# The attention half of an output projection by Strassen's algorithm (one core, fp32 products in three passes)

## The chip, the cores and the metric

One NeuronCore of a Trainium2 chip runs the whole program. The metric is device microseconds of one execution, lower is better. Engines are named as in the profile: PE (matrix products), DVE (vector), ACT (scalar), POOL (GpSimd), SP (it issues most DMAs).

## The reference

A hybrid encoder block on x (512 positions by 2048), cut to what matters here:

```
h   = rmsnorm(x, norm1_g)
z   = h @ w_in
attn = windowed_gqa(q, k, v, sink)        # 512 x 1024, 8 heads of 128
gm   = chunked_spatial_gating(zg, ...)    # 512 x 1024, 8 groups of 128
mix = concat(rmsnorm(attn, attn_out_norm_g), rmsnorm(gm, gmlp_out_norm_g))
x   = x + mix @ w_out                     # w_out: 2048 x 2048
x   = x + conv_ffn(rmsnorm(x, norm2_g), w_up, conv_w, conv_b, w_down)
out = rmsnorm(x, final_g)
```

The first 1024 rows of `w_out` meet the attention branch, the other 1024 the gating branch. All is float32.

## The kernel before

**Three passes.** Every float32 operand of a large product is split in two parts, `hi` (an ACT cast, `nc.scalar.copy`) and `lo` (a DVE subtraction), and `mm3` (lines 81 to 83) issues three 128x128 by 128x512 matmuls: hi by hi, hi by lo, lo by hi. Weights come from memory in tiles of 128x1024 (512 KB) into a ring of six buffers, the pool `raw`. Their split parts go into the pool `wp`, three buffers for `hi` and three for `lo`. `weights` (line 68) does it all for one tile: SP's load, ACT's cast, DVE's subtraction.

**Order of the program.** Input projection and attention; values of the gating branch; `u` projection (four steps of `tiles_A`, each followed by the gating of two groups); output projection; then an up projection and a down projection that run interleaved, the down one by Strassen's algorithm already (tiles `dp`); final norm.

**The stretch of the change.** `project(half, src, c, r)` (line 413) makes one block of 512 output columns: 4 tiles of weights, 4 row blocks, 96 matmuls into four PSUM banks (tiles `pj`), then one DVE instruction for each row block (line 427) that adds bank times row scale to the residual. Half 0 is attention (columns c = 0 to 3, scale `ra`), half 1 gating (scale `rg`). While half 0 runs, SP also loads the 16 residual blocks `x2[t][c]` of 128x512 (line 425). The attention activations are split once, `ats` (lines 363 to 369).

**What sets the order.** A framework builds the program, orders each engine's instructions by its own plan, and puts a semaphore wait where a tile is read or its buffer reused. Each engine runs its list in order, so one that waits holds up all behind it; SP's list of DMA issues too. The pool `big` has 64 slots of 128x512; a slot comes free when the last reader of its tile is done.

Of the kernel before, what the change touches and what calls it, by code (L numbers as in the profile page):

```python
# [24 lines left out]
H = 8  # L25
KV = 2
# [19 lines left out]


@with_exitstack
def hymba_block(ctx, tc, xT, x, w_in, w_up, w_out, w_down, wsT, cols, brow, frow, srow, rel, out):
# [163 lines left out]
    kk = {}  # L213
# [33 lines left out]
    pst = [psm.tile([P, 256], F32, tag="m", name=f"va_{t}") for t in range(NT)]  # L247
    for u in range(4):
        hi, lo = next_in()
        hv = hi.rearrange("p (k c) -> p k c", k=4)  # L250
        lv = lo.rearrange("p (k c) -> p k c", k=4)
        for t in range(NT):
            for k in range(4):
                kt = u * 4 + k
                a = tuple(z[:, t * P : (t + 1) * P] for z in xs[kt])
                mm3(pst[t], a, (hv[:, k, :], lv[:, k, :]), kt == 0, kt == KT - 1)
    for t in range(NT):
        if t % 2 == 0:
            vh, vl = slot(F32R, f"vah{t}"), slot(F32R, f"val{t}")
        hi, lo = (z[:, (t % 2) * 256 : (t % 2 + 1) * 256] for z in (vh, vl))  # L260
# [4 lines left out]
    at = [slot(F32, f"at{h}") for h in range(H)]  # L265
# [85 lines left out]
    for t in range(NT):  # L351
        for c in range(2):
            v = vg[2 * t + c].rearrange("p (g c) -> p g c", c=P)
            i = t * NG + 4 * c
# [5 lines left out]
        nc.sync.dma_start(ws[i], wsT[:, 4 * i : 4 * i + 4, :].rearrange("p g c -> p (g c)"))  # L360
        nc.sync.dma_start(gb[i], brow[i * S : (i + 1) * S].partition_broadcast(P))

    atg = [[oct.tile([P, 4, S], F32R, tag="oct", name=f"ats{z}{g}") for z in "hl"] for g in range(KV)]
    ats = []
    for h in range(H):
        hi, lo = (z[:, h % 4, :] for z in atg[h // 4])
        nc.scalar.copy(hi, at[h])
        nc.vector.tensor_tensor(lo, at[h], f(hi), op=ALU.subtract)
        ats.append((hi, lo))

    ra = row_stat(asq, 1024, "ra")
    ug = {}
# [13 lines left out]
    def gating(h):  # L386
        ps = pss.tile([P, S], F32, tag="s", name=f"gv{h}")
        for n in range(NT):
            v = vg[2 * n + h // 4][:, (h % 4) * P : (h % 4 + 1) * P]
            nc.tensor.matmul(ps[:, n * P : (n + 1) * P], v, ws[h // 4][:, (h % 4) * P : (h % 4 + 1) * P], start=True, stop=True)  # L390
        t = slot(F32, f"gt{h}")
        bb = gb[h // 4][:, (h % 4) * P : (h % 4 + 1) * P].unsqueeze(1).broadcast_to([P, NT, P])
        nc.vector.scalar_tensor_tensor(
            t.rearrange("p (n c) -> p n c", c=P), ps.rearrange("p (n c) -> p n c", c=P),
            col[:, C_GV + h : C_GV + h + 1], bb, op0=ALU.mult, op1=ALU.add)
        nc.vector.tensor_tensor(t, t, ug[h], op=ALU.mult)
        if h == 0:
# [12 lines left out]

    x2 = [[slot(F32, f"x2_{t}{c}") for c in range(4)] for t in range(NT)]

    def project(half, src, c, r):
        pst = [psm.tile([P, S], F32, tag="m", name=f"pj{half}{c}{t}") for t in range(NT)]
        for u in range(4):
            hi, lo = weights(w_out[(half * 4 + c) * 4 + u], f"o{half}{c}{u}")
# [12 lines left out]
    for c in range(4):  # L429
        project(0, ats, c, ra)  # L430
    rg = row_stat(gsq, 1024, "rg")
    gms = [split(gm[h], f"gm{h}s", scale=col[:, C_GM + h : C_GM + h + 1]) for h in range(NG)]
    ss2 = const.tile([P, 4 * NT], F32, name="ss2")
    hs = []
    for c in range(4):
        project(1, gms, c, rg)
# [271 lines left out]
    for t in range(NT):  # L708
# [19 lines left out]
        for c in (1, 0, 3, 2):  # L728
            o = x2[t][c]
# [21 lines left out]
def _layout(x, norm1_g, w_in, gmlp_v_norm_g, gmlp_ws, gmlp_b, attn_sink, attn_out_norm_g,  # L751
            gmlp_out_norm_g, w_out, norm2_g, w_up, conv_w, conv_b, w_down, final_g):
    x = np.asarray(x)[0]
    wi, wo, wu, wd = (np.asarray(a)[0] for a in (w_in, w_out, w_up, w_down))
    q, k, v = wi[:, :1024], wi[:, 1024:1280], wi[:, 1280:1536]
    u, gv = wi[:, 1536:2560], wi[:, 2560:]
    w1 = np.concatenate([
        _units(np.concatenate([k, q[:, :256]], 1), 512), _units(q[:, 256:512], 256), _units(v, 256),
        _units(q[:, 512:], 256), _units(gv, 512), _units(u, 256)])
    gu = np.concatenate([wu[:, :DFF].reshape(D, NCT, 1, P), wu[:, DFF:].reshape(D, NCT, 1, P)], 2)  # L760
    w2 = _units(gu.reshape(D, 2 * DFF), 256)
    w3 = np.concatenate([_units(wo[:1024], 512), _units(wo[1024:], 512)])
# [10 lines left out]
    return {  # L773
        "xT": np.ascontiguousarray(x.T).reshape(KT, P, S),
        "x": x,
        "w_in": w1, "w_up": w2, "w_out": w3, "w_down": w4,
        "wsT": np.ascontiguousarray(np.asarray(gmlp_ws)[0].transpose(2, 0, 1)),
        "cols": np.ascontiguousarray(cols),
        "brow": np.asarray(gmlp_b)[0].reshape(-1),
        "frow": np.asarray(final_g),  # L780
        "srow": np.asarray(attn_sink)[0],
        "rel": rel,
    }
# [17 lines left out]
```

## Time and profile before

| what | value |
|---|---|
| median of 3 runs | 1943.1 us (1942.53 to 1944.31) |
| the profiled execution | 1942.97 us, span 1941.2 us |
| PE busy in the span | 1929.4 us (99%) |
| DVE, ACT, POOL busy | 63%, 36%, 5% |
| attention's half of the projection | 364.4 to 451.6 us |
| DMA, mean over the span | 120 GB/s |

The span runs from the first to the last instruction; the execution's own time is 1.8 us more. The median of the runs is within 0.2 us of the profiled execution. Times of the trace are microseconds from the span's start.

### The profile page before, as it was taken

What the parts mean: (1) busy time and instruction counts of PE and PEld (TensorE: products, weight loads), DVE (VectorE), ACT (ScalarE), POOL (GpSimd) and SP (SyncE); (2) the same over time, 40 slices, a digit from 0 to 9 for tenths busy, and PEclk for the clock granted to TensorE, in tenths of its full rate; (3) what the DMA queues carried; (4) which work ended last, traced back from release to release, by engine and by line L of the source; (5) the groups of instructions that cost most, each with busy time, mean ns of one, the idle gap of its engine ahead of it and who ended that gap; (6) DMA issues with size and microseconds to landing.
All of it is one profiled execution on the core that took longest, in us unless ns stands there. A gap on an engine that the chain in (4) does not pass through costs nothing.

```text
span 1941.2 us, 22114 instructions
## 1 busy us (share of the span) xinstructions
PE 1929.4 (99%) x8776; PEld 1601.8 (83%) x8776; DVE 1219.1 (63%) x1652; ACT 694.7 (36%) x915; POOL 91.1 (5%) x105
## 2 busy tenths in 40 slices
PE   9999999999999999999999999999999999999998
PEld 8988888888888888888888888888888888888886
DVE  7476573444444767667566666676665757667857
ACT  6243442322332334333233333333333334333334
POOL 5001100100000000000000000000000000000000
PEclk9999999999999999999999999999999999999999
DMA  7212232522223344433444344434444344444432
GB/s 259 97 66 75 68 115 91 174 98 88 92 93 108 109 129 129 128 118 123 133 132 129 115 125 141 130 108 131 131 130 130 109 131 128 133 123 129 132 127 87
DMA packets 68104, 232.54 MB, mean 120 GB/s; under 512 B 7696, under 2 KB 7968, under 8 KB 68000
## 3 DMA queue, kind: packets, MB, share of 16 engines
q1 hardware_dynamic: 62064, 209.87, 31.8%
q0 software_dynamic: 5792, 20.99, 6.6%
q8 instruction: 68, 1.11, 0.2%
q10 hardware_dynamic: 144, 0.26, 0.0%
q14 instruction: 36, 0.29, 0.0%
HBM read 226.90 MB, written 4.19 MB: 119 GB/s over the span
## 4 chain that ended last, share of the span: by engine, by line
PE 98%; DVE 1%; ACT 0%; DMA 0%; issue 0%; ACTq 0%; POOL 0%; POOLq 0%; DVEq 0%
PE up L83 16%; PE up L82 16%; PE up L81 16%; PE dp L81 7%; PE dp L82 7%; PE dp L83 7%; PE pj L81 3%; PE pj L83 3%; PE pj L82 3%; PE g L82 2%; PE g L83 2%; PE g L81 2%; PE u L81 2%; PE u L83 1%; PE u L82 1%; PE vg_ps L81 1%
## 5 line engine op out<-in xcount | busy, mean ns | idle before, releaser
L83 PE MATMUL up<-h_h,lo_u 128*128 128x512 f32 x1408 | 547.9, 389 | 0.0
L81 PE MATMUL up<-h_h,hi_u 128*128 128x512 f32 x1408 | 547.9, 389 | 0.0
L82 PE MATMUL up<-h_l,hi_u 128*128 128x512 f32 x1408 | 547.8, 389 | 0.0
L82 PEld LDWEIGHTS up<-h_l,hi_u 128*128 128x128 f32 x1408 | 264.4, 188 | 54.8
L81 PEld LDWEIGHTS up<-h_h,hi_u 128*128 128x128 f32 x1408 | 264.4, 188 | 54.8
L83 PEld LDWEIGHTS up<-h_h,lo_u 128*128 128x128 f32 x1408 | 264.4, 188 | 54.7
L460 ACT CAST hi_u<-st_u 128x1024 fp32r<-128x1024 f32 x176 | 185.7, 1055 | 323.5 <-PE dp L83 180.6
L461 DVE TENSOR_TENSOR lo_u<-st_u,hi_u 128x1024 fp32r<-128x1024 f32 x176 | 215.2, 1223 | 116.8 <-ACT hi_u L460 116.8
L461 DVE TENSOR_TENSOR lo_b<-st_d,hi_b 128x1024 fp32r<-128x1024 f32 x60 | 73.4, 1223 | 145.6 <-ACT hi_b L460 145.6
L568 DVE TENSOR_TENSOR x<-x,dp 128x512 f32<-128x512 f32 x200 | 136.1, 682 | 1.4
L460 ACT CAST hi_b<-st_d 128x1024 fp32r<-128x1024 f32 x60 | 63.3, 1055 | 179.7 <-PE up L82 175.0
L77 DVE TENSOR_TENSOR lo_i<-st_i,hi_i 128x1024 fp32r<-128x1024 f32 (+1 forms) x57 | 72.0, 1264 | 70.8 <-ACT hi_i L76 70.7
L487 ACT ACTIVATE c<-a,col 128x512 f32<-128x512 f32 x88 | 71.2, 809 | 118.5 <-DVE a L484 118.4
L461 DVE TENSOR_TENSOR lo_t<-st_d,hi_t 128x1024 fp32r<-128x1024 f32 x40 | 48.9, 1223 | 88.6 <-ACT hi_t L460 88.6
L76 ACT CAST hi_i<-st_i 128x1024 fp32r<-128x1024 f32 (+1 forms) x57 | 58.8, 1032 | 119.8 <-PE u L82 38.7
L77 DVE TENSOR_TENSOR lo_o<-st_o,hi_o 128x1024 fp32r<-128x1024 f32 x32 | 39.2, 1225 | 95.5 <-ACT hi_o L76 95.5
L81 PE MATMUL dp<-hi_t,afs 128*128 128x512 f32 x240 | 93.4, 389 | 0.0
L82 PE MATMUL dp<-lo_t,afs 128*128 128x512 f32 x240 | 93.4, 389 | 0.0
L83 PE MATMUL dp<-hi_t,afs 128*128 128x512 f32 x240 | 93.4, 389 | 0.0
L549 POOL DMA_DIRECT2D st_t<-in_w_down x40 | 34.8, 869 | 1237.0 <-DMA st_t<-in_w_down 860.0
L489 DVE SCALAR_TENSOR_TENSOR c<-a,col,c 128x511 f32<-128x511 f32 x88 | 66.1, 751 | 41.5 <-ACT c L487 41.2
L460 ACT CAST hi_t<-st_d 128x1024 fp32r<-128x1024 f32 x40 | 42.2, 1054 | 109.0 <-PE up L82 105.2
(288 smaller groups left out, 3226.6 us busy)
## 6 DMA issues: line engine op xcount, KB each, us to landing
st_u<-in_w_up SPq DMA_DIRECT2D x176, 512.0 KB, 3.2
st_d<-in_w_down SPq DMA_DIRECT2D x60, 512.0 KB, 3.3
st_i<-in_w_in SPq DMA_DIRECT2D x55, 512.0 KB, 3.3
st_t<-in_w_down SPq DMA_DIRECT2D x40, 512.0 KB, 3.3
st_t<-in_w_down POOLq DMA_DIRECT2D x40, 512.0 KB, 5.4
st_o<-in_w_out SPq DMA_DIRECT2D x32, 512.0 KB, 3.2
xg<-in_xT SPq DMA_DIRECT2D x16, 256.0 KB, 6.4
x<-in_x SPq DMA_DIRECT2D x16, 256.0 KB, 5.6
```

Source lines behind the costliest of these rows:

```text
L76: nc.scalar.copy(hi[:, cs], st[:, cs])
L77: nc.vector.tensor_tensor(lo[:, cs], st[:, cs], f(hi[:, cs]), op=ALU.subtract)
L81: nc.tensor.matmul(ps, a[0], b[0], start=start, stop=False, skip_group_check=free)
L82: nc.tensor.matmul(ps, a[0], b[1], start=False, stop=False, skip_group_check=free)
L83: nc.tensor.matmul(ps, a[1], b[0], start=False, stop=stop, skip_group_check=free)
L460: nc.scalar.copy(hi, st)
L461: nc.vector.tensor_tensor(lo, st, f(hi), op=ALU.subtract)
L487: nc.scalar.activation(t, a, AF.Identity, scale=w[1], bias=col[:, C_CB + j * 44 + i : C_CB + j * 44 + i + 1])
L489: nc.vector.scalar_tensor_tensor(t[:, 1:], a[:, : S - 1], w[0], t[:, 1:], op0=ALU.mult, op1=ALU.add)
L549: nc.gpsimd.dma_start(t, src(*y), accum_op=ALU.add)
L568: nc.vector.tensor_tensor(d, d, ps, op=op)
```

## The change

Attention's half of the projection becomes two runs of `attn_out(m)`. Run m makes the output columns of blocks m and m + 2 by the Winograd form of Strassen's algorithm: rows in two halves (256 each), the 1024 inner elements in two halves of four heads, columns in two halves. Seven products stand where the plain form has eight. A product is two half-products of 12 matmuls (`mm3` four times, 128x512 each): 2 x 7 x 24 = 336 matmuls in place of 384. The products are, in order: `b11`, `t3`, `b21`, `t4`, `t1`, `t2`, `b22`.

- Weights: `b11`, `b21`, `b22` are quarters of the weights, loaded. `t3` and `t1` are a load plus a second DMA, issued by POOL, that adds another quarter (line 468 of the new file). `t2` and `t4` are DVE additions (line 478). `b11` and `t3` lie in the ring `raw` (two tiles of 512 KB each), the rest in slots of `big` (four loads of 256 KB each).
- Activations: `at_forms(k)` makes the seven forms for one pair of heads on DVE and ACT, in pieces of 128x256. Forms 0 and 1 follow the gating of u step 2, forms 2 and 3 that of step 3.
- Results: product 1 is copied to `acco` by ACT; `into` (line 502) adds PSUM times row scale to two residual blocks; `attn_sums` (line 542) adds `acco` later, within `project`, which now does the gating half only.
- Residual blocks: eight pairs, each just ahead of the product that needs it.

```
-    atg = [[oct.tile([P, 4, S], F32R, tag="oct", name=f"ats{z}{g}") for z in "hl"] for g in range(KV)]
-    for h in range(H):
-        nc.scalar.copy(hi, at[h])
-        nc.vector.tensor_tensor(lo, at[h], f(hi), op=ALU.subtract)
...
+    def at_forms(k):
+        c = S // 2
+        a11, a21, a12, a22 = at[k][:, :c], at[k][:, c:], at[4 + k][:, :c], at[4 + k][:, c:]
+        def put(name, v):
+            hi, lo = atf[name][k][:, :c], atf[name][k][:, c:]
+            nc.scalar.copy(hi, v)
+            nc.vector.tensor_tensor(lo, v, f(hi), op=ALU.subtract)
+        put("11", a11)
+        put("12", a12)
+        put("22", a22)
+        t = slot(F32, f"ats{k}")
+        d, e = t[:, :c], t[:, c:]
+        nc.vector.tensor_tensor(d, a11, a21, op=ALU.subtract)
+        put("s3", d)
+        nc.vector.tensor_tensor(e, a22, a21, op=ALU.subtract)
+        put("s1", e)
+        nc.vector.tensor_tensor(d, e, a11, op=ALU.add)
+        put("s2", d)
+        nc.vector.tensor_tensor(e, d, a12, op=ALU.subtract)
+        put("s4", e)
...
+        if q >= 2:
+            at_forms(2 * q - 4)
+            at_forms(2 * q - 3)
...
+        def plus(x_, y_, name, ring=False):
+            ts, parts = blocks(name, ring)
+            for t, s_ in zip(ts, chunks(*x_, len(ts))):
+                nc.sync.dma_start(t, s_)
+            for t, s_ in zip(ts, chunks(*y_, len(ts))):
+                nc.gpsimd.dma_start(t, s_, accum_op=ALU.add)
+            return parts
...
+        def product(a, ts, name, ps, start):
+            for kk in range(2):
+                hi = wp.tile([P, 1024], F32R, tag="whi", name=f"ohi_{name}{m}{kk}")
+                lo = wp.tile([P, 1024], F32R, tag="wlo", name=f"olo_{name}{m}{kk}")
+                for k in range(2):
+                    cs, st = slice(k * S, (k + 1) * S), ts[2 * kk + k]
+                    nc.scalar.copy(hi[:, cs], st)
+                    nc.vector.tensor_tensor(lo[:, cs], st, f(hi[:, cs]), op=ALU.subtract)
...
+        b11 = q(0, 0, True)
+        t3 = plus((1, 1), (0, 1), "t3", True)
+        residual(1, 1)
+        pa = bank(psm, "m", "op1")
+        product("11", b11, "b11", pa, True)
+        for t in range(2):
+            nc.scalar.copy(acco[m][t], pa[t])
+        b21 = q(1, 0)
+        residual(0, 0)
+        pb = bank(pss, "s", "op7")
+        product("s3", t3, "t3", pb, True)
+        into(1, 1, pb, nra)
+        t1 = plus((0, 1), (0, 0), "t1")
+        residual(1, 0)
+        product("12", b21, "b21", pa, False)
+        into(0, 0, pa, ra)
+        t2 = add(b11, t3)
+        t4 = add(b21, t2)
+        product("22", t4, "t4", pb, False)
+        into(1, 0, pb, ra)
+        b22 = q(1, 1)
+        residual(0, 1)
+        pa = bank(psm, "m", "op5")
+        product("s1", t1, "t1", pa, True)
...
-            if half == 0:
-                nc.sync.dma_start(x2[u][c], x[u * P : (u + 1) * P, c * S : (c + 1) * S])
+            if u == 0:
+                attn_sums(c)
...
-    for c in range(4):
-        project(0, ats, c, ra)
+    for m in range(2):
+        attn_out(m)
...
+    w3 = wo[:1024].reshape(2, 4, P, 2, 2, 512).transpose(4, 0, 3, 2, 1, 5).reshape(8, P, 2048)
+    w3g = _units(wo[1024:], 512)
```

**How it moves instructions, place 1: SP's list where the projection begins.** In the names `st_o` are weights of the projection before, `x2` residual blocks (row, column), `owq` and `owt` the new weight tiles: the digits of `owt310` are t3, run 1, tile 0, of `owq1000` b21, run 0, tile 0. Before, SP had:

```order
L75 DMA st_o020_3311<-in_w_out 128x1024
L425 DMA x2_00_3027<-in_x 128x512
L425 DMA x2_10_3031<-in_x 128x512
L425 DMA x2_20_3035<-in_x 128x512
L425 DMA x2_30_3039<-in_x 128x512
L425 DMA x2_01_3028<-in_x 128x512
```

At the same place it now has:

```order
L466 DMA owt310_3453<-in_w_out 128x1024
L466 DMA owt311_3454<-in_w_out 128x1024
L474 DMA x2_22_3109<-in_x 128x512
L474 DMA x2_32_3113<-in_x 128x512
L460 DMA owq1000_3173<-in_w_out 128x512
L460 DMA owq1001_3174<-in_w_out 128x512
L460 DMA owq1002_3175<-in_w_out 128x512
L460 DMA owq1003_3176<-in_w_out 128x512
L474 DMA x2_00_3099<-in_x 128x512
```

The weights of product 3 (`owq1000` to `owq1003`) stand behind the ring loads of the other run's t3, whose second one, `owt311`, needs the ring buffer that t3 of run 0 (`owt301`) leaves.

**Place 2: SP's list ahead of the third product of run 1.** The list before has no such tiles; after `x2_33` it held only `st_o` loads. Now:

```order
L75 DMA st_o02_3896<-in_w_outg 128x1024
L75 DMA st_o03_3926<-in_w_outg 128x1024
L460 DMA owq1010_3501<-in_w_out 128x512
L460 DMA owq1011_3502<-in_w_out 128x512
L460 DMA owq1012_3503<-in_w_out 128x512
L460 DMA owq1013_3504<-in_w_out 128x512
L474 DMA x2_01_3100<-in_x 128x512
L474 DMA x2_11_3104<-in_x 128x512
L466 DMA owt110_3551<-in_w_out 128x512
```

`st_o03`, a weight tile of the gating half, takes the ring buffer of `owt311` (t3 of run 1), and b21 and t1 of run 1 (`owq101x`, `owt11x`) are queued behind it.

**Place 3: PE's list at the start of product 4 of run 1.** `op710` and `op711` are the two banks of products 2 and 4, `op510` the first bank of product 5, `ohi` and `olo` the split weights:

```order
L81 MATMUL op710_3511<-ohi_t410_3611,atf22_2383 128x512
L81 MATMUL op711_3512<-ohi_t410_3611,atf22_2383 128x512
L81 MATMUL op510_3659<-ohi_t110_3661,atfs10_2384 128x512
L82 MATMUL op710_3511<-olo_t410_3612,atf22_2383 128x512
L83 MATMUL op710_3511<-ohi_t410_3611,atf22_2383 128x512
```

One matmul of product 5, which reads t1's first tile, stands in the list after two of product 4's 24.

## Rows read from the trace of the kernel before

**Rows 1.** The page, part 1: busy time, share of the span, instructions of each engine.

```profile
PE 1929.4 (99%) x8776; PEld 1601.8 (83%) x8776; DVE 1219.1 (63%) x1652; ACT 694.7 (36%) x915; POOL 91.1 (5%) x105
```

**Rows 2.** Windows: length, busy us (instructions) of each engine, PE clock, DMA share, GB/s.

```profile
364.40:451.60 87.20, 87.20 (x389) 72.22 (x387) 37.29 (x43) 22.00 (x25) 3.10 (x2) 1.00 0.44 145
...
364.40:386.00 21.60, 21.60 (x98) 17.92 (x97) 9.63 (x13) 6.27 (x8) 3.10 (x2) 1.00 0.83 275
386.00:451.60 65.60, 65.60 (x292) 54.30 (x291) 27.66 (x32) 15.73 (x17) 0.00 (x0) 1.00 0.31 102
```

**Rows 3.** Tile pj: ns min/median/max of one, first and last start in us.

```profile
L81 PE MATMUL pj<-hi_o,atsh x128: 389/389/476, 364.4 to 450.9; 128*128 128x512 f32 x128
L82 PE MATMUL pj<-lo_o,atsh x128: 389/389/395, 364.7 to 451.1; 128*128 128x512 f32 x128
L83 PE MATMUL pj<-hi_o,atsl x128: 389/389/393, 365.0 to 451.3; 128*128 128x512 f32 x128
```

**Rows 4.** Groups of instructions by form: busy us, mean ns of one, idle before.

```profile
L81 PE MATMUL dp<-hi_t,afs 128*128 128x512 f32 x240 | 93.4, 389 | 0.0
...
L568 DVE TENSOR_TENSOR accu<-accu,dp 128x512 f32<-128x512 f32 x80 | 53.8, 684 | 1.1
...
L427 DVE SCALAR_TENSOR_TENSOR x<-pj,ra_r,x 128x512 f32<-128x512 f32 x16 | 11.6, 747 | 3.2 <-PE pj L83 3.2
...
L610 DVE TENSOR_TENSOR x<-x,dn 128x256 f32<-128x256 f32 x8 | 3.3, 418 | 1.1 <-PE dn L83 0.9
...
L521 ACT CAST afs<-s 128x512 fp32r<-128x512 f32 x40 | 24.8, 620 | 31.2 <-DVE s L512 31.2
```

**Rows 5.** DVE's timeline: start, us, what.

```profile
316.69 1.23 DVE L77 TENSOR_TENSOR lo_i<-st_i,hi_i 128x1024 fp32r<-128x1024 f32 x1
...
364.95 0.74 DVE L393 SCALAR_TENSOR_TENSOR gt<-gv,col,gb 128x512 f32<-128x512 f32 x1
...
367.19 0.69 DVE L396 TENSOR_TENSOR gt<-gt,u 128x512 f32<-128x512 f32 x1
```

**Rows 6.** SP's timeline of DMA issues.

```profile
267.32 0.42 SPq L361 DMA_DIRECT2D gb<-in_brow  x1
267.84 0.38 SPq L360 DMA_DIRECT2D ws<-in_wsT  x1
268.31 0.38 SPq L361 DMA_DIRECT2D gb<-in_brow  x1
273.26 39.57 SPq L75 DMA_DIRECT2D st_i<-in_w_in  x8
317.94 47.45 SPq L75 DMA_DIRECT2D st_o<-in_w_out  x9
365.44 5.25 SPq L425 DMA_DIRECT2D x<-in_x  x9
```

**Rows 7.** The page, part 6: DMA issues, KB each, median us from issue to landing.

```profile
st_t<-in_w_down POOLq DMA_DIRECT2D x40, 512.0 KB, 5.4
st_o<-in_w_out SPq DMA_DIRECT2D x32, 512.0 KB, 3.2
```

**Rows 8.** Line 425, the residual loads (last line of the answer).

```profile
DMA to landing us min/median/max: 4.7/5.6/6.2
```

**Rows 9.** ACT's timeline in attention's half, and SP and POOL at one accumulating load.

```profile
375.64 1.05 ACT L76 CAST hi_o<-st_o 128x1024 fp32r<-128x1024 f32 x1 [4.39 <-PE pj L83]
...
610.97 0.33 SPq L466 DMA_DIRECT2D st_t<-in_w_down  x1
...
614.96 0.88 POOL L549 DMA_DIRECT2D st_t<-in_w_down  x1 [79.13 <-DVE c L490]
```

**Rows 10.** Windows at the end of the program, columns as in rows 2.

```profile
1930.00:1932.00 2.00, 1.74 (x15) 1.53 (x13) 1.59 (x6) 1.13 (x4) 0.00 (x0) 1.00 0.36 120
1932.00:1934.00 2.00, 0.00 (x0) 0.00 (x0) 1.25 (x7) 0.51 (x2) 0.00 (x0) 0.92 0.00 0
1934.00:1936.00 2.00, 0.00 (x0) 0.00 (x0) 1.86 (x6) 1.15 (x2) 0.00 (x0) 0.50 0.00 0
```

More of the change, by code (lines that the diff above doesn't have):

```diff
@@ L48, in hymba_block @@
 @with_exitstack
-def hymba_block(ctx, tc, xT, x, w_in, w_up, w_out, w_down, wsT, cols, brow, frow, srow, rel, out):
+def hymba_block(ctx, tc, xT, x, w_in, w_up, w_out, w_outg, w_down, wsT, cols, brow, frow, srow, rel, out):
     nc = tc.nc
@@ L361, in hymba_block @@
         nc.sync.dma_start(gb[i], brow[i * S : (i + 1) * S].partition_broadcast(P))
-    atg = [[oct.tile([P, 4, S], F32R, tag="oct", name=f"ats{z}{g}") for z in "hl"] for g in range(KV)]
-    ats = []
-    for h in range(H):
-        hi, lo = (z[:, h % 4, :] for z in atg[h // 4])
-        nc.scalar.copy(hi, at[h])
-        nc.vector.tensor_tensor(lo, at[h], f(hi), op=ALU.subtract)
-        ats.append((hi, lo))
+    atf = {}
+    for name in ("11", "s3", "12", "22"):
+        t = oct.tile([P, 4, S], F32R, tag="oct", name=f"atf{name}")
+        atf[name] = [t[:, k, :] for k in range(4)]
+    for name in ("s1", "s2", "s4"):
+        atf[name] = [slot(F32R, f"atf{name}{k}") for k in range(4)]
+    def at_forms(k):
[18 more added lines that the diff above has]
+        put("s4", e)
     ra = row_stat(asq, 1024, "ra")
@@ L408, in hymba_block @@
         gating(2 * q + 1)
+        if q >= 2:
+            at_forms(2 * q - 4)
+            at_forms(2 * q - 3)
     x2 = [[slot(F32, f"x2_{t}{c}") for c in range(4)] for t in range(NT)]
-    def project(half, src, c, r):
-        pst = [psm.tile([P, S], F32, tag="m", name=f"pj{half}{c}{t}") for t in range(NT)]
+    nra = const.tile([P, NT], F32, name="nra")
+    nc.vector.tensor_scalar_mul(nra, ra, -1.0)
+    acco = [[slot(F32, f"acco{m}{t}") for t in range(2)] for m in range(2)]
+    c = S // 2
@@ new lines, in attn_out, with chunks, blocks, q @@
+    def attn_out(m):
+        def chunks(kh, nh, n):
+            a, w = w_out[(m * 2 + kh) * 2 + nh], 2048 // n
+            return [a[:, i * w : (i + 1) * w] for i in range(n)]
+        def blocks(name, ring):
+            if ring:
+                ts = [raw.tile([P, 1024], F32, tag="raw", name=f"ow{name}{m}{k}") for k in range(2)]
+                return ts, [t[:, k * S : (k + 1) * S] for t in ts for k in range(2)]
+            ts = [slot(F32, f"ow{name}{m}{k}") for k in range(4)]
+            return ts, ts
+        def q(kh, nh, ring=False):
+            ts, parts = blocks(f"q{kh}{nh}", ring)
+            for t, s_ in zip(ts, chunks(kh, nh, len(ts))):
+                nc.sync.dma_start(t, s_)
[3 more added lines that the diff above has]
+            for t, s_ in zip(ts, chunks(*x_, len(ts))):
+                nc.sync.dma_start(t, s_)
+            for t, s_ in zip(ts, chunks(*y_, len(ts))):
+                nc.gpsimd.dma_start(t, s_, accum_op=ALU.add)
+            return parts
+        def residual(th, nh):
+            for t in range(2):
+                r, cb = 2 * th + t, 2 * nh + m
+                nc.sync.dma_start(x2[r][cb], x[r * P : (r + 1) * P, cb * S : (cb + 1) * S])
+        def add(xs_, ys_):
+            for x_, y_ in zip(xs_, ys_):
+                nc.vector.tensor_tensor(x_, x_, y_, op=ALU.add)
+            return xs_
+        def product(a, ts, name, ps, start):
[6 more added lines that the diff above has]
+                    nc.vector.tensor_tensor(lo[:, cs], st, f(hi[:, cs]), op=ALU.subtract)
+                for t in range(2):
+                    for k in range(2):
+                        form = atf[a][2 * kk + k]
+                        z = tuple(form[:, i * c + t * P : i * c + (t + 1) * P] for i in range(2))
+                        w = tuple(z_[:, k * S : (k + 1) * S] for z_ in (hi, lo))
+                        mm3(ps[t], z, w, start and kk == 0 and k == 0, kk == 1 and k == 1, True)
+        def bank(pool, tag, name):
+            return [pool.tile([P, S], F32, tag=tag, name=f"{name}{m}{t}") for t in range(2)]
+        def into(th, nh, ps, r):
+            for t in range(2):
+                d = x2[2 * th + t][2 * nh + m]
+                nc.vector.scalar_tensor_tensor(d, ps[t], r[:, 2 * th + t : 2 * th + t + 1], d, op0=ALU.mult, op1=ALU.add)
+        b11 = q(0, 0, True)
[3 more added lines that the diff above has]
+        product("11", b11, "b11", pa, True)
+        for t in range(2):
+            nc.scalar.copy(acco[m][t], pa[t])
[16 more added lines that the diff above has]
+        product("s1", t1, "t1", pa, True)
+        into(1, 1, pa, nra)
+        pb = bank(pss, "s", "op6")
+        product("s2", t2, "t2", pb, True)
+        for t in range(2):
+            nc.vector.tensor_tensor(acco[m][t], acco[m][t], pb[t], op=ALU.subtract)
+        product("s4", b22, "b22", pa, False)
+        into(0, 1, pa, nra)
@@ L415, in project, with attn_sums @@
+    def attn_sums(cb):
+        m = cb % 2
+        for th, r in ((0, nra), (1, nra)) if cb >= 2 else ((1, ra),):
+            for t in range(2):
+                d = x2[2 * th + t][cb]
+                nc.vector.scalar_tensor_tensor(d, acco[m][t], r[:, 2 * th + t : 2 * th + t + 1], d,
+                                               op0=ALU.mult, op1=ALU.add)
+    def project(src, c, r):
+        pst = [psm.tile([P, S], F32, tag="m", name=f"pj{c}{t}") for t in range(NT)]
         for u in range(4):
-            hi, lo = weights(w_out[(half * 4 + c) * 4 + u], f"o{half}{c}{u}")
+            hi, lo = weights(w_outg[c * 4 + u], f"o{c}{u}")
@@ L435, in hymba_block @@
     for c in range(4):
-        project(1, gms, c, rg)
+        project(gms, c, rg)
         for t in range(NT):
@@ L775, in _layout @@
         "x": x,
-        "w_in": w1, "w_up": w2, "w_out": w3, "w_down": w4,
+        "w_in": w1, "w_up": w2, "w_out": w3, "w_outg": w3g, "w_down": w4,
         "wsT": np.ascontiguousarray(np.asarray(gmlp_ws)[0].transpose(2, 0, 1)),
```

1 line of the change is left out of this document (removed).

## The prediction, made blind

> **What bounds the kernel now.** The page first: PE is busy for 1929.4 of 1941.2 us [rows 1], so what counts is PE's own work and any wait put in its way. Then the windows of the stretch that changes: in 364.4 to 451.6 PE is busy for all of its 87.2 us at full clock, DVE for 37.3, ACT for 22.0, the DMA engines for 44% [rows 2]. The reader is to see that the stretch waits for nothing: loads, casts and subtractions are ready early, and the room they leave is what the change spends. DMA is not even there: 83% busy at 275 GB/s up to 386, 31% after [rows 2]. Then tile pj for the price of a matmul: 3 x 128 start between 364.4 and 451.3 [rows 3]; 87.2 / 384 = 0.227 us each. A row's 389 ns is longer, because matmuls overlap.
>
> The sum is against the profiled execution, 1943.0 us, which agrees with the median of 1943.1 to 0.2. A measurement of this kernel tells 0.2% from no change, 3.9 us: below 1939.2 is faster, above 1947.0 slower.
>
> **PE's work.** 336 matmuls stand for 384. They have the shape of those before, and the Strassen products already in the kernel, tile dp, show the same 389 ns [rows 4], so 0.227 us holds: 48 x 0.227 = **10.9 us less**; the stretch becomes 76.3 us if nothing waits. No other PE instruction is added. I count time from 364.4; a half-product of 12 matmuls takes 2.72 us, and half-product n (0 to 27) starts at 2.72 n.
>
> **Ahead of the stretch.** at_forms 0 and 1 add 22 small DVE instructions and their casts, after the gating of the third u step. In the windows of these steps DVE has more than half its time free: its 10 us in 23 show in the timeline as one subtraction per 5.4 us. I cost this at nothing; PE's cover is two weight tiles ahead, and if it went, some 3 us of small operations would show. The first products are loaded and split in that time too.
>
> **Product 3 of run 0 (wait A).** From gt6 at 0.55 [rows 5], DVE has in order up to the second `lo` of t301: 4 gating instructions (2 of 747 ns, 2 of 690), 3 subtractions of 128x512 (684) and 5 of 128x256 (418) [rows 4, 5]: 2.9 + 2.1 + 2.1 = 7.1, to 7.6; back-to-back starts overlap a little, so I take 7.0. SP wakes within 0.1 us of such a subtraction (316.69 + 1.23, then an issue at 317.94 [rows 5, 6]) and issues owt311, behind which stand two residual loads and b21 (place 1), at 0.49 us apiece, the spacing of single issues [rows 6]: owq1000 leaves at 8.5. The nearest row to such a train of 256 KB loads is line 425: 4.7 to 6.2 us to landing, median 5.6 [rows 8]; I take 5.2, since only three loads are just ahead. It lands at 13.7, its cast takes 0.62 [rows 4], and PE could start at 14.3. It wants to at 4 x 2.72 = 10.9. **Wait 3.4 us.** Bounds: landing after 3.2, as a lone 512 KB load does [rows 7], leaves 1.4; landing after 6.2 [rows 8] plus 1.7 that the POOL additions in flight may take leaves 6.1. Two other things come out at much the same point, and so would not vanish with a faster DMA: DVE's forms 2 and 3, ahead of the two `into` and the first `lo` of b21, and ACT's copies into acco, which product 3 needs before it overwrites its bank; by the sum of their instructions both end near 11 to 12.
>
> **Product 5 of run 1 (wait B).** Place 2: `st_o03` waits for the last `lo` of owt311, half-product 17. With three buffers in wp, its casts start when half-product 14 is off PE, 15 x 2.72 = 40.8 plus a lag of 0.36 (before, a cast starts at 375.64, four half-steps of 2.72 after 364.4 plus that lag [rows 9]). Two casts and the last `lo`: 41.2 + 1.2 + 0.7 = 43.1. Then SP issues st_o03, four parts of b21, two residual blocks; owt110 is seventh after it, 43.1 + 7 x 0.49 = 46.5. Landing 5.2: 51.7. POOL's addition follows 0.7 after a landing (610.97 + 3.3 to 614.96 [rows 9]) and takes 5.4 for 512 KB [rows 7], of which half the data is some 0.7, an estimate from the 350 GB/s and more that the busy slices of this stretch move: 4.7 for 256 KB. That is 57.1, with the cast 57.7. In PE's list (place 3) the matmul that reads it stands at 54.9, in the middle of product 4, and PE keeps its order: **wait 2.8 us**. b21 of run 1 itself comes within 1 us of its time, and that lies inside this wait. Bounds: landing in 3.2 gives 0.8; landing in 6.2 and an addition of 5.4 gives 4.5.
>
> **Small ones.** `into` of product 3 stands on DVE ahead of a `lo` of product 4, in both runs: a few tenths of PE, 0.3 in all. The additions t2 and t4, the rest of `into` and `attn_sums` lie beside PE's work. SP's and POOL's other issues wait for nothing of theirs: t1 of run 0 is issued from 12 on and wanted at 25.
>
> **Sum.** 1943.0 - 10.9 + 3.4 + 2.8 + 0.3 = **1938.6 us**, 0.23% below the median. With its bounds, 1936 to 1941.5.
>
> **Rivals.** *Loads land sooner.* The stretch has fewer bytes in its first 20 us than before, when line 425 gave its 5.6. With 3.2 for each load A is 1.4, B 0.8: 1943.0 - 10.9 + 1.4 + 0.8 + 0.3 = 1934.6. Against it: the loads come in trains, and POOL's additions run beside them. The Trainium skill's page "DMA: Bandwidth & Descriptors", section "Anatomy of one DMA", gives one transfer some 2.0 us and its bytes at 436 GB/s, 2.6 us for 256 KB; a lone 512 KB load agrees (3.2 by both), line 425 does not; by that rule A would be 0.8, B nothing, and the time an estimated 1933.
>
> *DVE becomes the bound.* From gt6 to the last `lo` ahead of the gating half DVE has 115 instructions where the whole stretch had 43 [rows 2]: 16 of 128x256, 68 of 684 ns, 31 of 747 [rows 4]: 6.7 + 46.5 + 23.2 = 76.4 us, no less than PE's 76.3. Back to back it does this in some 68. If instead it idles in waits A and B and for each PSUM bank that `into` reads, the stretch is 76.4 plus 8 to 9: gain 2 to 3, some 1940.5. Against it: subtractions run up to two half-products ahead.
>
> *The waits cost PE its clock; this one ends slower.* At the end of the program PE's last matmul is over before 1932, and the granted clock is 1.00 up to there, 0.92 as the mean of the next 2 us, 0.50 after [rows 10]: after some two idle us it fell from 2.4 to 1.2 GHz. Waits A and B are longer than that. Every us of work at 1.2 GHz costs half a us. If the clock stays low as long as the waits lasted, 6.2 us, the loss is 3.1: 1941.7, no measurable gain. Past 17 us of work at the low clock, of the stretch's 76, it eats the 4.4 of gain and 3.9 more: slower, say 1948. No row shows how soon the clock comes back. The Trainium skill's page "TensorE: Matmul & The Clock Gate", section "HAM oscillation — how this bites in real kernels", tells of kernels whose wait for a DMA, again and again, sent the next group of matmuls off at half the clock. By that rule each of the two waits is followed by a slow group; the end of this trace agrees that idling lowers the clock.
>
> That the change doesn't do what it says I exclude: the lists hold 336 such matmuls.
>
> **Chances.** Forecast 0.50; loads land sooner 0.17; DVE the bound 0.13; clock 0.20, of which 0.08 past the point where it is slower. Faster: 0.62 of the forecast's range lies below 1939.2, 0.31; with 0.17 and some 0.04 of the other two, 0.52. Slower 0.08, within 0.2% 0.40. The range leaves out half a tenth below and about one and a half above: 1933.5 to 1943.5.
>
> **What would show it.** Right: about 336 matmuls on op tiles at 389 ns; PE idle some 3 us before the first matmul of op10 that reads b21, released by ACT's cast behind a DMA; some 3 us before the early op51 matmul, behind an addition by POOL; granted clock 1.00; the gating half as long as before. Wrong: a clock row below 1.00 in the stretch (third rival); no waits over 1 us (first); many waits of some tenths for `lo` tiles with DVE near 100% (second); or a wait in a place that I cost at nothing, the u steps or the start of the gating half.

## The result, and the profile after

The changed kernel takes 1957.1 us (median of 3 runs, 1956.3 to 1957.3; a fourth, at a mean clock of 0.65 of full speed, is left out), against 1942.8 before: ratio 1.0071 (95%: 1.0057 to 1.0085). It is slower by 14 us, which had a chance of 0.08, and lies above the forecast's range. The profiled execution took 1957.12 us, 14.1 more than that of before.

The page of the changed kernel: the span, and each engine's busy time, share and instructions.

```profile
span 1955.3 us, 22270 instructions
PE 1929.6 (99%) x8728; PEld 1597.8 (82%) x8728; DVE 1271.4 (65%) x1765; ACT 718.1 (37%) x979; POOL 101.1 (5%) x117
```

PE is busy as long as before (1929.4 [rows 1]) although it has 48 matmuls fewer, and that is the first thing to distrust: at half the clock the same work counts nearly double. The windows of the stretch show where. It starts at 366.2 now (364.4 before); columns as in [rows 2].

```profile
366.20:378.20 12.00, 11.42 (x51) 8.76 (x49) 11.81 (x23) 5.65 (x13) 3.94 (x3) 1.00 0.52 132
378.20:383.40 5.20, 0.14 (x1) 0.00 (x0) 1.73 (x3) 1.32 (x3) 0.87 (x1) 0.93 0.98 266
383.40:389.20 5.80, 5.71 (x13) 4.42 (x14) 4.99 (x8) 3.17 (x7) 0.00 (x0) 0.50 1.06 312
389.20:397.40 8.20, 8.20 (x36) 6.51 (x34) 3.90 (x6) 1.60 (x3) 3.03 (x4) 0.98 1.08 344
397.40:406.00 8.60, 5.96 (x21) 3.56 (x21) 4.35 (x7) 3.52 (x8) 0.47 (x1) 1.00 0.63 156
406.00:435.70 29.70, 29.47 (x128) 23.52 (x126) 27.19 (x44) 12.98 (x23) 2.00 (x3) 1.00 0.55 183
435.70:441.40 5.70, 0.00 (x0) 0.00 (x0) 2.78 (x5) 0.95 (x2) 1.04 (x2) 0.94 1.07 276
441.40:447.20 5.80, 5.71 (x14) 4.45 (x14) 2.07 (x3) 1.89 (x5) 0.50 (x1) 0.50 0.71 155
```

Two windows with PE idle (second and seventh), each followed by one at 0.50 of the clock, in which only 13 or 14 matmuls run in 5.8 us; at 1.00 that time holds 25. The DMA engines are full (0.98 to 1.08) from 378 to 397 and around 438. DVE is busy through the first 12 us. The waits of PE from 366 to 470 (total, times, longest, us), then the rows of PE's timeline at which they end (start, duration; in brackets the idle time and what ended it):

```profile
PE op L81 <- ACT ohi_t L487: 7.8, 2, 5.8
PE op L81 <- ACT ohi_b L487: 5.2, 1, 5.2
PE op L82 <- DVE olo_t L488: 0.7, 3, 0.2
PE op L81 <- ACT atfs L377: 0.6, 1, 0.6
```

```profile
383.49 1.22 PE L81 MATMUL op<-ohi_b,atf 128*128 128x512 f32 x2 [5.15 <-ACT ohi_b L487]
385.36 0.63 PE L81 MATMUL op<-ohi_b,atf 128*128 128x512 f32 x1
389.79 0.40 PE L81 MATMUL op<-ohi_b,atf 128*128 128x512 f32 x1
400.92 0.50 PE L81 MATMUL op<-ohi_t,atfs 128*128 128x512 f32 x1 [1.98 <-ACT ohi_t L487]
441.49 0.79 PE L81 MATMUL op<-ohi_t,atfs 128*128 128x512 f32 x1 [5.80 <-ACT ohi_t L487]
```

**A** is the wait for `b21` ahead of product 3 of run 0, **B** that of the early matmul of product 5 in run 1, both where they were forecast. **C**, the wait for `t1` of run 0 (1.98 us and some of 0.2), is one that I had costed at nothing. A row of 0.63 us (385.36) is a matmul at 1.2 GHz, one of 0.40 (389.79) at 2.4. The account, against the 1943.0 of before, from the starts of the matmuls (one starts 0.227 us after the other where nothing is late):

| where | us |
|---|---|
| 48 matmuls fewer | -10.9 |
| forms 2 and 3 late (second product of run 0) | +0.9 |
| wait A | +5.3 |
| low clock after A, 383.5 to 389.2 | +2.9 |
| wait C | +4.2 |
| small waits for `lo` | +0.7 |
| wait B | +6.0 |
| low clock after B, 441.5 to 447.2 | +2.9 |
| low clock at the program's start (last section) | +1.8 |
| sum, of 14.1 measured | +13.8 |

Why `b21` is late is in SP's list of issues (some residual loads between are left out here):

```profile
367.28 7.46 SPq L466 DMA_DIRECT2D owt<-in_w_out  x2
375.80 2.21 SPq L460 DMA_DIRECT2D owq<-in_w_out  x4
380.82 3.00 SPq L466 DMA_DIRECT2D owt<-in_w_out  x4
406.97 16.61 SPq L75 DMA_DIRECT2D st_o<-in_w_outg  x4
426.47 3.30 SPq L466 DMA_DIRECT2D owt<-in_w_out  x4
```

The two loads of run 1's `t3` (`owt310`, `owt311`) hold the list until 374.7, for a ring buffer that the last `lo` of `t301` frees; `b21`'s four loads (375.80) and `t1`'s (380.82) stand behind them with nothing of their own to wait for: their slots are free, as experiment 1 shows. From 406.97 to 423.6 the gating weights hold it in the same way, and `t1` of run 1 (426.47) stands behind those. POOL then adds to `t1`:

```profile
389.94 2.64 POOL L468 DMA_DIRECT2D owt<-in_w_out  x3 [8.37 <-DMA owt<-in_w_out]
397.01 0.86 POOL L468 DMA_DIRECT2D owt<-in_w_out  x1 [4.43 <-PE op L83]
441.02 0.87 POOL L468 DMA_DIRECT2D owt<-in_w_out  x1 [4.66 <-issue]
```

The DMA issues from 366 to 450 (KB each, median us to landing) show that the tiles of 256 KB land late:

```profile
owq<-in_w_out SPq DMA_DIRECT2D x16, 256.0 KB, 6.2
owt<-in_w_out SPq DMA_DIRECT2D x8, 256.0 KB, 7.3
owt<-in_w_out POOLq DMA_DIRECT2D x8, 256.0 KB, 7.7
```

### The profile page after: what moved, and what is told of

It reads as the page before. It is cut to its first block, busy times and chain, and to the rows that moved or that the text cites. A ratio compares the mean times of both kernels' runs of the same rounds, so it can differ in the third digit from the quotient of the medians.

```text
span 1955.3 us, 22270 instructions
## 1 busy us (share of the span) xinstructions
PE 1929.6 (99%) x8728; PEld 1597.8 (82%) x8728; DVE 1271.4 (65%) x1765; ACT 718.1 (37%) x979; POOL 101.1 (5%) x117
## 4 chain that ended last, share of the span: by engine, by line
PE 96%; DMA 2%; DVE 1%; ACT 0%; issue 0%; SPq 0%; ACTq 0%; POOL 0%; POOLq 0%; DVEq 0%
PE up L82 16%; PE up L81 16%; PE up L83 16%; PE dp L83 6%; PE dp L82 6%; PE dp L81 6%; PE g L81 2%; PE g L83 2%; PE g L82 2%; PE pj L81 1%; PE u L81 1%; PE pj L83 1%; PE u L83 1%; PE u L82 1%; PE pj L82 1%; PE vg_ps L81 1%
## 5 line engine op out<-in xcount | busy, mean ns | idle before, releaser
L592 ACT CAST hi_t<-st_t 128x1024 fp32r<-128x1024 f32 x40 | 42.2, 1055 | 98.5 <-PE up L82 94.7
```

Of the source, the lines that this page charges most:

```text
L592: nc.scalar.copy(hi, st)
```

## The experiments

My theory after the result: A, B and C come from issues that stand ready in SP's list behind issues that wait, and from `t1`'s second DMA; the low clock follows the long waits. Rivals: the DMA engines are simply full; DVE, which must end the forms before the freeing `lo`, is late; the order of PE's list puts B where it is. All were run in 5 rounds; ratios are to the kernel before, with 95% intervals. Diffs are against the changed kernel.

Beside the time of the whole program it helps to have that of the stretch alone, from the first matmul on an `op` tile to the first on `pj`, in the profiled execution: the 1.8 us at the program's start, which some executions have and some not (last section), are then left out. The changed kernel takes 99.6 us for it, and experiments 1 to 11 take 90.3, 86.3, 99.6, 97.0, 99.2, 107.4, 92.0, 88.1, 88.1, 79.3 and 76.3.

**1. Run 1's `t3` loads leave SP's list.**

```
-                nc.sync.dma_start(t, s_)
+                (nc.gpsimd if ring and m == 1 else nc.sync).dma_start(t, s_)
```

> Edit: the two plain loads of t3 of run 1 (owt310, owt311) are issued by POOL instead of SP, so that the loads of b21 and the residual blocks no longer stand behind them on SP. Theory (place in SP's list): b21 is issued some 10 us or more earlier, the 5.2 us wait before product 3 of run 0 goes, and with it the 2.9 us that the low clock cost behind it; the 0.9 us in product 2 for forms 2 and 3 stays. Waits for t1 may grow by 1 or 2 us, since PE comes to them earlier. About 1949.5 us. Rival (the DMA engines' bandwidth alone sets it, whatever the order of issue): at least 3 us of the wait and the low clock stay, 1954 us or more.

Measured: 1946.4 us, ratio 1.0015 (1.0006 to 1.0024), 10.7 below the changed kernel; the stretch is 9.2 shorter. SP's list, and the waits of PE:

```profile
352.81 1.75 SPq L460 DMA_DIRECT2D owq<-in_w_out  x4
```

```profile
PE op L81 <- ACT ohi_t L487: 5.9, 2, 5.5
PE op L81 <- ACT ohi_b L487: 1.4, 2, 1.2
```

`b21` leaves at 352.8 instead of 375.8. A shrinks to 1.2 and the clock stays at 1.00 there; C shrinks to 1.5 by the spacing of the rows, since `t1` left early too. The figure expected was undercut by 3.1: 2.8 of it by rows is C, and the 1.8 of the program's start, which this execution did not have, may be in it as well. B, behind the gating weights, stays at 5.5.

**2. `t1` without its second DMA.**

```
-            for t, s_ in zip(ts, chunks(*y_, len(ts))):
+            for t, s_ in zip(ts, chunks(*y_, len(ts)) if ring else []):
```

> Edit: the second half of t1 is left out in both runs (the eight additions that POOL issues as DMAs), so t1 is one plain load; the rest is as in the change. Theory (the addition comes behind the load and takes 6.5 to 10 us more): the 4.2 us of waits for t1 in run 0 go, the 6.0 us wait for t1 in run 1 goes and with it the 2.9 us at the low clock; the wait before product 3 of run 0 stays at 5 us. About 1944 us. Rival (bytes alone): 2 MB less, some 5 us at 390 GB/s, spread over all the waits, 1952 us.

Measured: 1942.3 us, ratio 0.9996 (0.9987 to 1.0005). B and C are gone but for tenths, A is not (5.0):

```profile
PE op L81 <- ACT ohi_b L487: 5.5, 2, 5.0
```

By the starts of the matmuls the additions cost 13.3 us of the stretch: C 4.2, B 5.1 (0.8 is left there), the clock after B 2.9, and 1.3 of the clock after A, where 7 matmuls are slow here instead of 13; the small waits differ by some tenths. This version leaves out half of `t1`, so it tells what the additions cost, not a way to save them.

**3. PE kept at work through A**, with 22 matmuls that nobody reads.

```
+        if m == 0:
+            fill(22, atf["s3"][3])
         product("12", b21, "b21", pa, False)
```

> Edit: 22 matmuls of 128x512 that nobody reads stand on PE between products 2 and 3 of run 0, where PE otherwise idles; they add 5.0 us of PE work. Theory (the low clock behind that wait comes from idling): b21 comes when it came, the idle stretch is filled, the clock stays at 1.00 there, and the time falls by the 2.9 us that the low clock cost, to 1954.3 us, though work is added. Rival (the low clock has another cause, DMA or DVE load): the clock still falls, and the time stays at 1957 us or rises.

Measured: 1955.9 us, 1.0069 (1.0057 to 1.0082). The windows (columns as above):

```profile
376.40:381.40 5.00, 5.00 (x23) 4.14 (x23) 2.12 (x4) 1.66 (x4) 0.87 (x1) 1.00 0.93 299
393.40:396.00 2.60, 0.03 (x1) 0.00 (x0) 0.00 (x0) 0.50 (x1) 0.29 (x1) 1.00 1.10 262
397.00:403.00 6.00, 5.99 (x13) 3.96 (x14) 1.41 (x3) 1.91 (x4) 0.00 (x0) 0.50 0.60 154
```

With PE busy the clock stays at 1.00 after A, as expected. But product 3 is then sooner done, PE waits 2.74 us for `t1`, and the clock falls there. The 2.9 us moved by one product. So it is the idling that lowers the clock, and behind one late load stands the next: time won at A is lost at C, and the stretch is as long as before (99.6).

**4. B's place in PE's list.** Six unread matmuls ahead of product 5 of run 1 make the planner put its early matmul behind product 4.

```
+        if m == 1:
+            fill(6, atf["22"][3])
         product("s1", t1, "t1", pa, True)
```

> Edit: 6 matmuls of 128x512 that nobody reads are put ahead of product 5 of run 1; the planner then sets them after the first two matmuls of product 4, where the early matmul of product 5 stood, and that one goes behind product 4. Theory (the early matmul holds up 22 matmuls that are ready): they run in the 6.0 us in which PE waited for t1; the wait shrinks to 2 us or less (the fourth part of t1, added last, may take its place), the clock does not fall there; the 6 fillers cost nothing or 1.4 us. About 1950 us, 1952 with the fourth part late. Rival (the order of PE's list does not matter, product 4 itself waits): no gain, 1957 us or above.

Measured: 1951.6 us, 1.0044 (1.0031 to 1.0056), as expected. B's 5.8 is gone: 0.5 us at most is left there in one piece (the 1.5 below is at C), and 8 slow matmuls in place of 14. Another 8 are slow behind C, where the changed kernel had none; they take back some 1.6 us. (The profiled execution took 1953.1 us, 1.5 above the median.)

```profile
PE op L81 <- ACT ohi_b L487: 4.3, 1, 4.3
PE op L81 <- ACT ohi_t L487: 2.7, 3, 1.5
```

**5. `t1` as one load and an addition by POOL itself.**

```
-        t1 = plus((0, 1), (0, 0), "t1")
+        t1 = q(0, 1)
+        for k in range(4):
+            nc.gpsimd.tensor_tensor(t1[k], t1[k], b11[k], op=ALU.add)
```

> Edit: t1 is one plain load of a quarter plus four additions of the first tiles (b11) by POOL, in place of a second DMA that adds; the output is the same. In SP's list owt310 and owt311 then stand behind b21, t1, b22 and the residual blocks of run 0, and two of the four gating weights behind the loads of run 1. Theory (t1's second DMA and the place of blocked issues in SP's list make the waits): as after moving t3 to POOL's queue, 0.9 us for forms 2 and 3 and 1.8 us for b21 stay; the waits for t1 go in both runs, no wait is longer than 1.5 us and the granted clock stays at 1.00. About 1937 us. Rival (POOL's additions are too slow, or slow DVE beside them): t1 is late again by some us, 1942 us or more.

Measured: 1953.7 us, 1.0051 (1.0039 to 1.0064): a miss. The timelines of POOL, and of DVE in the same time:

```profile
370.24 6.00 POOL L518 TENSOR_TENSOR owq<-owq,owq 128x512 f32<-128x512 f32 x4
```

```profile
370.48 1.79 DVE L488 TENSOR_TENSOR olo_t<-owt,ohi_t 128x512 fp32r<-128x512 f32 x1
372.19 2.93 DVE L378 TENSOR_TENSOR atfs<-ats,atfs 128x256 fp32r<-128x256 f32 x2
375.04 1.48 DVE L389 TENSOR_TENSOR ats<-ats,at 128x256 f32<-128x256 f32 x1
```

A `lo` takes 1.79 us instead of 0.68, two subtractions of 128x256 take 2.93 instead of 0.75, a third 1.48 instead of 0.41 ([rows 4] for the `lo` and one subtraction): each takes about what one POOL addition takes (6.00 / 4). That falls on the forms and `lo` tiles for which PE, and SP's list, wait. PE now waits 4.4 us for a form, 3.9 for `t4` and 3.4 for a `lo`. The Trainium skill, page "SBUF — State Buffer", section "SBUF: two separate sides", says that a DVE instruction with two inputs in SBUF and a POOL instruction that reads SBUF exclude each other for a whole instruction. The rows agree.

**6. Most forms later:** forms 11, 12, 22 and s3 of all heads after u step 2, s1 after product 3, s2 and s4 after product 4, so that DVE ends the freeing `lo` sooner.

```
+        if q == 2:
+            for k in range(4):
+                at_forms(k, 0)
...
+        if m == 0:
+            for k in range(4):
+                at_forms(k, 1)
```

> Edit: of the seven forms, the four that products 1 to 4 need are made after u step 2 for all heads; s1 follows after product 3, s2 and s4 after product 4. Loads and t1 as in the change. Theory (22 DVE instructions of forms 2 and 3 stand ahead of the last lo of t301, which SP waits for): the 0.9 us of wait in product 2 goes, the loads of b21 are issued some 3 us earlier against PE and the 5.2 us before product 3 shrink to 2 or 3; the waits for t1 stay. About 1952 us. Rival (the DMA engines are full, b21 lands when it lands): the wait before product 3 only takes over the 0.9 us, 1956 us.

Measured: 1963.7 us, 1.0101 (1.0088 to 1.0115): a miss, the slowest of all.

```profile
PE op L81 <- ACT ohi_t L494: 12.6, 3, 6.1
PE op L81 <- ACT ohi_b L494: 4.3, 2, 3.9
PE op L82 <- DVE olo_t L495: 4.1, 1, 4.1
```

The wait for forms went and A fell to 3.9, but the planner now gives run 0 an early matmul of product 5 as well: it waits 5.7 us for `t1` with the rest of product 4 behind it. After it the `lo` of `t1` is late by 4.1, since DVE has the moved forms to make.

**7. Experiments 5 and 6 together.**

> Edit: both: t1 by one load and POOL's additions, and the forms as late as they are needed. Theory: the waits that were left in run 0 (0.9 us in product 2, 1.8 us before product 3) go as well; what stays are some tenths for lo tiles, and DVE's work of 76 us in a stretch of 78 becomes the next bound. About 1934.5 us. Rival (DVE is already the bound): many waits of some tenths for lo tiles and forms s1, s2 and s4, and 1937 us or more.

Measured: 1947.9 us, 1.0019 (1.0010 to 1.0028): a miss again, by 13 us. A is gone. One wait of 6.1 and one of 3.4 stay (for `t1` at an early matmul of product 5 in run 0, and for a `lo` on DVE).

**8. The waiting issues on ACT:** run 1's `t3` and the third and fourth gating weights are issued by ACT.

```
-                nc.sync.dma_start(t, s_)
+                (nc.scalar if ring and m == 1 else nc.sync).dma_start(t, s_)
...
-            hi, lo = weights(w_outg[c * 4 + u], f"o{c}{u}")
+            hi, lo = weights(w_outg[c * 4 + u], f"o{c}{u}", 1, (nc.scalar,) if c == 0 and u >= 2 else ())
```

> Edit: the four loads that wait for a buffer of the ring and stood ahead of others in SP's list are issued by ACT instead: owt310 and owt311, and the gating weights st_o02 and st_o03. Nothing else is changed (t1 with its second DMA, forms, additions). The planner's order of PE then has no early matmul of product 5 in run 1. Theory (SP's list holds up loads whose slots are free): run 0 as with t3 on POOL's queue, 0.9 us for forms, 1.8 us for b21, 1 to 2 us for t1; in run 1 t1 is loaded and added in time, its 5.7 us wait goes and with it the last fall of the clock. About 1938.5 us. Rival (DVE's order and amount of work is the next bound, as in the two kernels with POOL's additions): t1's wait in run 1 only gives way to waits for lo of t4, 1942 us or more.

Measured: 1944.5 us, 1.0008 (0.9999 to 1.0017): no change against the kernel before, and 6 us above what was expected. No wait is over 2.1 us. But SP's list is still held, now by two residual loads:

```profile
369.33 7.77 SPq L474 DMA_DIRECT2D x<-in_x  x2
```

Their issue waited for the landing of the `owt` loads that ACT had issued: ACT's two landed at 369.25 and 376.71, and the two residual loads were issued at 369.33 and 376.77, each with the landing semaphore that ACT's load had used. That the shared semaphores are the tie fits these times, and was not tried apart. `t1` of run 0 left at 377.2; in experiment 1 it left at 355.6.

**9. Experiment 8 with the forms earlier:** 11, 12, 22 and s3 after u step 1, s1, s2 and s4 after u step 2, so that the gating of the last u step is no longer mixed with them.

```
+        if q in (1, 2):
+            for step in ((0,), (1, 2))[q - 1]:
+                for k in range(4):
+                    at_forms(k, step)
```

> Edit: the same four loads on ACT, and all forms made earlier: the four that need no s1 after u step 1, s1, s2 and s4 after u step 2, none beside POOL's last additions of the gating. Theory: the 0.9 us in product 2 and most of the 1.8 us before product 3 go too; t1 in run 0 keeps 1 to 2 us or takes over some of it (an early matmul of product 5 stands in product 4 there). About 1936 us. Rival (PE's order decides: that early matmul waits for t1 and holds up product 4): 4 us or more there and a fall of the clock, 1941 us or more.

Measured: 1944.3 us, 1.0008 (0.9999 to 1.0016): the rival's number. A and the wait for forms are gone, the rest is lost again at one place: an early matmul of product 5 in run 0 waits 8.3 us for `t1`, in one piece.

**10. The waiting issues on POOL.** Run 1's `t3` goes into `big` (four loads, no ring buffer to wait for), and the gating weights of the first block are issued by POOL. Two lines, not tried apart:

```
-        t3 = plus((1, 1), (0, 1), "t3", True)
+        t3 = plus((1, 1), (0, 1), "t3", m == 0)
...
-            hi, lo = weights(w_outg[c * 4 + u], f"o{c}{u}")
+            hi, lo = weights(w_outg[c * 4 + u], f"o{c}{u}", 1, (nc.gpsimd,) if c == 0 else ())
```

> Edit, two lines: t3 of run 1 lies in slots of big, not in the ring, so that its loads wait for no ring buffer; and the four gating weights of the first block are issued by POOL, not SP. SP's list then holds no load that waits for a lo of these products, POOL's additions for t1 of run 0 come ahead of those for run 1, and PE's list has no early matmul of product 5. Theory (issues that wait, standing ahead of issues that could go, made the long waits): 0.9 us for forms 2 and 3 and some 2 us before product 3 of run 0 stay, t1 is in time in both runs, the clock falls at no place or for 1.5 us at most. 1943 - 10.9 + 4 = 1936 us. Rival (DMA bandwidth or DVE is the next bound): 3 us or more of other waits, 1940 us or more.

Measured: 1935.4 us (1935.0 to 1936.9), ratio 0.9960 (0.9948 to 0.9972): 21.7 below the changed kernel and 7.7 below the one before, as expected; the stretch is 20.2 shorter. In PE's list no early matmul of product 5 is left (in experiments 8 and 11 neither), so B's place in that list has gone together with the late issues. The waits of PE of over 0.2 us:

```profile
PE op L81 <- ACT ohi_b L487: 1.2, 1, 1.2
PE op L81 <- ACT atfs L377: 0.6, 1, 0.6
```

**11. Experiment 10 with the earlier forms of experiment 9.**

> Edit: the same two lines, and the forms made earlier (those without s1 after u step 1, s1, s2 and s4 after u step 2). Theory: the waits for forms and before product 3 go too, as they did when the forms were early and four loads on ACT; some tenths are left: 1943 - 10.9 + 1.5 = 1933.5 us. Rival (DVE's work per product is the next bound): waits of some tenths for lo tiles add up to 3 us or more, 1936 us or more.

Measured: **1932.2 us** (1931.9 to 1934.0), ratio 0.9945 (0.9932 to 0.9959), the best version; 1933.5 was expected. Its windows:

```profile
364.40:374.00 9.60, 9.60 (x45) 7.99 (x45) 7.26 (x9) 5.49 (x11) 6.67 (x7) 1.00 1.05 391
384.00:394.00 10.00, 10.00 (x46) 8.28 (x45) 8.07 (x13) 4.58 (x8) 3.72 (x5) 1.00 1.10 290
364.00:444.00 80.00, 80.00 (x362) 66.44 (x361) 73.04 (x114) 40.70 (x68) 16.17 (x18) 1.00 0.71 218
```

PE waits for nothing; the stretch takes 76.25 us, 336 x 0.227. And the DMA engines are as full as ever (1.05 and 1.10). The trace's summary of the tile `owq`, for its 12 loads issued between 364 and 445, tells how late they land (least, median, most, us):

```profile
DMA to landing us min/median/max: 6.6/11.4/13.1
```

That settles the rival of the full DMA engines: loads that take 11.4 us, twice the 5.2 that I forecast, cost nothing here, where they are issued early enough. DVE runs 73.0 of 80 us and is not the bound either.

## Why the prediction was wrong, step by step

- **PE's work** was right: 10.9 us less, and experiment 11 shows it bare (1932.2; 1943.0 - 10.9 = 1932.1).
- **Wait A** had its place and its releaser right, and its size too small: 3.4 forecast, 5.3 measured (the bounds reached 6.1). Issue at 9.6 after the stretch's start instead of 8.5: from 365.91 DVE took 8.5 us instead of the 7.0 of my sum, because two subtractions of 128x256 took 1.5 us each beside POOL's gating additions (the timeline of all engines):

```profile
368.66 3.23 POOL L425 TENSOR_TENSOR gsq<-gsq,gsq 128x512 f32<-128x512 f32 x2 [19.96 <-ACT gsq L424]
369.23 1.52 DVE L385 TENSOR_TENSOR ats<-at 128x256 f32<-128x256 f32 x1
370.67 1.51 DVE L387 TENSOR_TENSOR ats<-at,at 128x256 f32<-128x256 f32 x1
```

  Landing took 6.9 to 7.3 instead of 5.2. Product 3 itself was wanted 1.1 later, by the wait for forms and the small ones: 3.4 + 1.1 + 1.9 - 1.1 = 5.3. The term that I took from [rows 8] was mis-sized: those loads ran with nothing beside them that adds in memory (that this alone makes the difference was not tried).
- **Wait B** likewise: 2.8 forecast, 6.0 measured, above my bound of 4.5. The issue of `owt110` came out as worked: 46.5 after 364.4 is 410.9, and with the 15.1 of delay by then (the account without B, its clock and the small waits, which come later) 426.0; measured 426.47. The load took 6.8 (5.2 forecast), its addition 7.0 (4.7).
- **C is the step that failed outright**: "SP's and POOL's other issues wait for nothing of theirs: t1 of run 0 is issued from 12 on and wanted at 25." That the loads wait for nothing of their own is true, and 13 us looked like cover. But the loads were issued from 14.6 on and took 7.8 to 8.5, and POOL's additions 6.7 to 10.4 after that: the third landed 20.9 us after the first load's issue (391.3 + 10.4 - 380.8), and the fourth was issued only at 397.01, when the first had landed. Cost: 4.2. I never summed this chain, though the one beside it (B) has the same links.
- **"I cost this at nothing"** was said of forms 0 and 1, and rightly (the u steps take as long as before). Forms 2 and 3 have no term of their own in the sum, and cost 0.9 in product 2.
- **The clock** I gave as a rival, with chance 0.20 and 3.1 us; it is not one. It comes on top of the forecast when waits no longer than the forecast's own lower the clock, as the 2.74 us of experiment 3 did, and it cost 5.8. Nor is it what made the change slower by itself: the 0.08 for "slower" were given for more than 17 us of work at the low clock, and the two windows at 0.50 are 11.6 us long. The mechanism was in [rows 10]; the mistake was to put it beside the sum instead of into it, and to give half the chance to a sum without it. The Trainium skill's page "TensorE: Matmul & The Clock Gate", section "HAM oscillation — how this bites in real kernels", says of a kernel whose waits for a DMA came again and again, that each time the matmuls after one start at half the clock. The two windows at 0.50 after A and B agree; the one after C, at 1.00, does not show it.
- **"DVE becomes the bound"** and **"loads land sooner"** fell: no wait for DVE was over 0.3 us in the changed kernel, and the loads of 256 KB took 6.2 to 7.8 in the median, none from 366 to 450 less than 4.5.
- **The bounds** of the two waits add up to 1934.6 to 1943.0 us, wider than the 1936 to 1941.5 that the sum was given; the measured time lies outside both.

So the waits, with the clock that they cost, came to 22.9 us (0.9 + 5.3 + 2.9 + 4.2 + 0.7 + 6.0 + 2.9), where 6.5 was forecast. What made them is shown by experiments 1, 2 and 10: loads that stand late in SP's list, and behind them POOL's additions (10 alone takes away 20.2 us of the stretch, with the same bytes, sums and forms), while the forms' place, worth 3.1 between 10 and 11, is second. How much of B is the late `t1` and how much the place of the early matmul in PE's list is not told apart: experiment 4 moved only that matmul and gained 5.6 us by the medians, of the 8.9 of B and its clock, and experiments 8, 10 and 11 changed both. Not tried: 1 and 2 together, and the earlier forms with SP's list as it was.

## What to carry to other kernels

Read an issue list as you read an engine: for each load, find the first issue ahead of it that waits for a buffer, and take that buffer's release as the load's earliest time; a list that mixes ring buffers with free slots can hold back the loads of the free slots, here by some 21 us (`b21` was issued 9.6 us after the start of the stretch, in experiment 1 11.7 us before it). Sum every chain of load, addition, cast to the matmul that reads it, also where ten us of cover seem to be there, and add to any long wait of PE the slow matmuls that follow it. When such a wait is found, move the issue to another queue before you try to make the transfer or the work behind it cheaper: here the first brought up to 20.2 us of the stretch, and experiments 5 to 7, which tried the second, 7.5 at best. The queue must be one that no other ready load waits for: on ACT's, in experiment 8, the same kind of move brought 11.5.

## What the runs showed of the hardware that I had not expected

- **The price of one wait** can't be read off its length. After C's 1.98 us of idling the granted clock was 1.00; after the 2.74 us of experiment 3 it was 0.50 for some 13 matmuls, most of which started 0.43 us apart instead of 0.227. In experiment 4 the waits in C's place are shorter, 0.75 and 1.48 with two of 0.2, and yet 8 matmuls behind them ran at 1.2 GHz:

```profile
398.55 0.50 PE L81 MATMUL op<-ohi_t,atfs 128*128 128x512 f32 x1 [1.48 <-ACT ohi_t L487]
400.41 0.63 PE L83 MATMUL op<-ohi_t,atfs 128*128 128x512 f32 x1
```

  Nor does the number of slow matmuls follow the wait: 13 after A (5.15 us) and after B (5.80) in the changed kernel, 7 after A in experiment 2 (5.02) and after B in experiment 3 (5.72). Why was not found.
- **DVE beside POOL** (experiment 5): only instructions with both inputs in SBUF became longer. One that reads PSUM took 0.75 us at 374.70 in experiment 7, while POOL was adding.
- **POOL's adding DMAs.** In both runs the fourth of 256 KB was issued 4.4 to 4.7 us after POOL was done with the third, 0.3 us after the first had landed (397.01 after 396.71, 441.02 after 440.72), and in experiment 1 likewise (430.39 after 430.08). What holds it was not tried.
- **The start of the program.** The matmuls from 6.2 to 10.2 us ran at 1.2 GHz in this execution of the changed kernel, and at 2.4 GHz from 7.6 in that of before (first row the changed kernel, second the one before):

```profile
7.67 0.63 PE L82 MATMUL g<-x_l,hi_i 128*128 128x512 f32 x1
7.62 0.40 PE L83 MATMUL g<-x_h,lo_i 128*128 128x512 f32 x1
```

It does not look like the change's: of the twelve profiled executions with the change four have it (the changed kernel and experiments 6, 9 and 10) and eight not, and of 21 runs of the kernel before on one chip some took 1942.5 to 1943.1 and some 1944.5 to 1944.9, a gap of about the same 1.8 us.
